# Layer 1's input projection: eight of its fifteen weight blocks by seven half-block products a pair, and its other weights split ahead in layer 0

## The chip, the cores and the metric

One core of a Trainium2 chip runs the whole kernel. The metric is the device time of one execution, in microseconds (us); the figure of a kernel is the median of its runs. The engines are TensorE (PE, matrix products), VectorE (DVE), ScalarE (ACT), GpSimd (POOL) and SyncE (SP). Here SP issues every large transfer, in one queue, and 16 DMA engines carry them out.

## What is computed

The reference is a decoder trunk of two layers over 1024 tokens and 1024 channels, in float32:

```
for l in range(2):
    h = rmsnorm(x, attn_norm[l])
    proj = h @ w_in[l]            # 1824 columns: q, kv and rotary key of a latent attention,
                                  # three parts of a gated convolution, a pooling input,
                                  # q, k, v of a sliding-window attention
    y_a, y_b, y_c, y_d = mla_attention(..), short_gated_conv(..), multiscale_pool(..), swa_sink_attention(..)
    x = x + (concat of the four groups, each rms-normed) @ w_o[l]
    gate, up = split(rmsnorm(x, ffn_norm[l]) @ w_gate_up[l])
    x = x + (silu(gate) * up) @ w_down[l]
return rmsnorm(x, final_norm)
```

## The kernel before

Everything is kept transposed: 128 channels on the partitions, tokens along the row, in two halves of 512 tokens (`HT`), so an activation block is 128 x 512 and there are 8 channel blocks (`NK`). Weights are 128 x 128 tiles.

**Split precision.** TensorE is fed with the type float32r. Each float32 operand is split into a high part (ACT copies and rounds it, L286 or L218) and a low part (DVE subtracts, L287 or L219), and each product is three matmuls, high x high, high x low and low x high, all in `mm3` (L275). So every weight that is used costs one load, one ACT pass and one DVE pass before the matmuls.

**Order of the work, layer by layer.** The mixer stage begins with the input projection: 15 blocks of 128 output columns (q 0-1, k 2, v 3, convolution 4-9, latent q 10-11, latent kv 12, pooling input 13-14) and a small rotary key block. `project` (L460) takes a block's split weights from `weights` (L206), which are loaded one or two blocks ahead through `take` and `ahead` (L249-256), and `proj` (L444) does for each token half 8 x 3 matmuls of 128x512. The evacuation multiplies by the row norm `ratt`, whose rsqrt is known only at the end of the layer before. Between the projections the units of the windowed attention are put (`swa_some`, L666). Then come the latent attention (`keys`, `queries`, `values`, `scores`, `mix_values`), the output projection in parts (`out_some`), and at the end the blocks of `w_o` for the latent group (`wa`, L1318).

**Feed-forward.** Gate and up are already done by Strassen's scheme in Winograd's form: two output blocks, two halves of the channels and two halves of the tokens make a 2 x 2 block product, done with seven half-size products in place of eight. The combinations of activations are made by `combine` (L1132), those of the weights in `GateUp.sums` and `sum4`. A loop at L1523 runs over 22 blocks `f`; each is seven `product` calls of four channel blocks, with DVE and ACT work for the next block woven in. The down projection (loop L1647) is 28 units, seven combinations (`order`, L1423) of four output pairs, each unit 33 matmuls; its weights `dn_raw` are loaded two units ahead, its activations come back from memory (`dn_acts`), and the sums of its weights were made during gate and up by `dn_sums` (L153). At its end `done` (L1612) splits the new `x` into the next layer's `hh`, stores it to `xs`, and adds its squares for the norm.

**Norms.** `SumSq.rnorm` sums squares over the partitions with a matmul by a matrix of ones: in float32 (L345) or, with `parts=True`, split in two float32r matmuls (L340).

**Memory on chip.** Large tiles live in 47 places of 128 x 1024 elements (`Slots`, L56), handed out in program order; a place that is handed out again makes its new writer wait for its last reader.

**What sets the order on each engine.** `arrange` (L1894) is a planner that runs over the program with prices for each instruction and writes out a fixed order for every engine and for SP's queue. The rank of an instruction in the program, moved by the numbers of the table `MOVED` (L2025), is its priority.

Of the kernel before, what the change touches and what calls it, by code (L numbers as in the profile page):

```python
# [55 lines left out]
class Slots:  # L56
# [9 lines left out]

    def pair(self, dt):
# [25 lines left out]
class View:  # L93
# [11 lines left out]

    def ap(self, i):
        assert self.s.dt[i // 2] == self.dt
        return self.s.cur[i // 2][:, i % 2, :]
# [7 lines left out]
def trunk_kernel(ctx: ExitStack, tc: tile.TileContext, ins, out):  # L116
# [26 lines left out]
    nffn = cpool.tile([P, L * NK], F32, name="nffn")  # L143
    act.preload_act_table_set("natural_log_exp_and_others")
# [3 lines left out]
    xr = dpool.tile([NK, P, S], F32, name="xr")  # L148
    ad = [dpool.tile([P, NG * HT], F32, name=f"ad{n}") for n in range(7)]

# [55 lines left out]
    def weights(src, n):  # L206
        if n > 2 * P:
            s = F.pair()
            raw = F.ap2(s)
            sp.dma_start(raw[:, :n], src)  # L210
            hi, lo = (R.ap2(i) for i in ring_next())
            F.free_pair(s)
        else:
            raw = wpool.tile([P, 2 * P], F32, name="vraw", tag="vraw")
            sp.dma_start(raw[:, :n], src)
            hi = wpool.tile([P, 2 * P], F32R, name="vhi", tag="vhi")
            lo = wpool.tile([P, 2 * P], F32R, name="vlo", tag="vlo")
        act.copy(hi[:, :n], raw[:, :n])  # L218
        dve.tensor_tensor(out=lo[:, :n], in0=raw[:, :n], in1=rd(hi[:, :n]), op=ALU.subtract)  # L219
        return hi, lo  # L220

# [17 lines left out]

    def expect_layer(l):  # L240
        for m in ((2, 3, 0) if l else ()) + (4, 5, 6, 1, 13, 14, 10, 11, 12, None, 7, 8, 9):
            if m is None:
                expect(rope_weights, l)
            else:
                expect(weights, ins["w_in"][l, m], 2 * HT)
        for d in range(NK):
            expect(weights, ins["w_o"][l, d, :, 2 * P :], 6 * P)
# [190 lines left out]
    for l in range(L):  # L438
        if l == 0:
            expect_layer(0)  # L440
        sums = dn_sums(l)

# [17 lines left out]
        def project():  # L460
            w = take()
            pp = [proj(w, t) for t in range(2)]
            ahead()
# [29 lines left out]

        if l == 0:
# [12 lines left out]
            for i in range(L):  # L507
                for o, c, n in ((nsink, PC_SINK, 8), (nffn, PC_FFN, NK)):
# [7 lines left out]
        else:  # L516
            wk = take()
            pk = [proj(wk, 0, "s")]
            wv = take()
            pv_ = [proj(wv, 0, "s")]  # L520
            pk.append(proj(wk, 1))
            pv_.append(proj(wv, 1, "s"))
            w = take()
            pq = [proj(w, 0, "s"), proj(w, 1, "t")]
        ahead()
        kk = [[R.pair(), R.pair()] for _ in range(2)]
        for t in range(2):
            f = tmp()
            mul_to(f, pk[t], r_of(t))
            for g, own, oth in ((0, hd, tl), (1, tl, hd)):  # L530
                k1, k2 = R.ap(kk[g][0] + t), R.ap(kk[g][1] + t)
                act.copy(k1[own], f[own])
                act.copy(k1[oth], f[own])
                dve.tensor_tensor(out=k2[own], in0=f[own], in1=rd(k1[own]), op=ALU.subtract)
                dve.tensor_tensor(out=k2[oth], in0=f[own], in1=rd(k1[own]), op=ALU.subtract)
        vs = [[R.half(), R.half()] for _ in range(2)]
        for t in range(2):
            f = tmp()
            mul_to(f, pv_[t], r_of(t))
            p = ps("t")  # L540
            for j in range(4):
                pe.transpose(p[:, j * P : (j + 1) * P], f[:, j * P : (j + 1) * P], ident)
            pv = p.rearrange("p (j g d) -> p j g d", j=4, g=2)
            for g in range(2):
                o = R.ap(vs[g][t]).rearrange("p (j h d) -> p j h d", j=4, h=2)
                act.copy(o[:, :, 0, :], pv[:, :, g, :])
            for g in range(2):
                o = R.ap(vs[g][t]).rearrange("p (j h d) -> p j h d", j=4, h=2)
                dve.tensor_tensor(
                    out=o[:, :, 1, :], in0=pv[:, :, g, :], in1=rd(o[:, :, 0, :]), op=ALU.subtract  # L550
                )

        swa_q(0, pq)
        ytiles("d")
# [126 lines left out]
        def group_scale(g):  # L681

            sg = SumSq(2 * P)
            for t in range(2):
                for c in range(2):
                    sg.add(t, F.ap(y[g][c][t]))
                r = sg.rnorm(t)
# [5 lines left out]
        mixed = {}  # L693

# [10 lines left out]
        def conv(ct):  # L705

            z = F.pair()
            pp = project()
            for t in range(2):
                mul_to(F.ap(z + t), pp[t], r_of(t))  # L710
            yield
            pp = project()
            for t in range(2):
                f = tmp()
                mul_to(f, pp[t], r_of(t))
                mul_to(F.ap(z + t), F.ap(z + t), f)
# [13 lines left out]
            F.free_pair(z)  # L730
            yield
# [8 lines left out]
        for _ in conv(0):  # L740
            swa_some(3)
        swa_q(1, project())


        ytiles("c")
        sw = R.half()
        raw = wpool.tile([P, 2 * P], F32, name="vraw", tag="vraw")
# [1777 lines left out]
```

## Time and profile before

| what | value |
|---|---|
| median of 3 runs | 2054.27 us (2053.95 to 2055.91) |
| the profiled execution | 2055.59 us, of which the span of the trace is 2053.8 us |
| granted TensorE clock | 0.997 of full speed |
| busy: PE, PE's weight loads, DVE, ACT | 2036.9, 1675.5, 1600.7, 981.4 us |
| bytes moved by DMA | 289.74 MB, mean 141 GB/s, 41.8% of the 16 engines' time |
| layer 0's gate and up, down | about 421 to 806 us, 807 to 1016 us of the span |
| layer 1's mixers | about 1016 to 1430 us of the span |

How to read it: an engine's busy time is the part of the span in which at least one of its instructions runs. Matmuls overlap one another, so a single one lasts 389 ns while the next begins long before its end; what one costs is the step from one start to the next. A line number is that of the statement that issues the instruction, and where a helper issues it (L275, L286, L287) the tile names tell the places apart: `u` are the 47 places, `ps_...` are PSUM banks, `in_...` are inputs in memory, and `qd`, `ad`, `xr`, `xs`, `xp` are scratch in memory.

### The profile page before, as it was taken

To read this page: it belongs to the slowest core of one execution; us is meant where nothing else is said; L and a number is where in the kernel's file an instruction comes from. 1 tells how busy PE (TensorE), PEld (TensorE's weight loads), DVE (VectorE), ACT (ScalarE), POOL (GpSimd) and SP (SyncE) were. 2 spreads that over 40 slices of the span, in tenths; PEclk is the share of its full clock that TensorE was granted. 3 is DMA by queue.
4 is the path that set the end of the run, shared out by engine and by line. 5 is a ranking of instruction groups with operands and counts; after the bars stand their busy time and mean duration, and the time that the engine had idled before them with its cause. 6 is when DMAs were issued, how large, how long until landed. Compare 5 with 4: busy or idle time off the path is not lost.

```text
span 2053.8 us, 26024 instructions
## 1 busy us (share of the span) xinstructions
PE 2036.9 (99%) x9418; PEld 1675.5 (82%) x9418; DVE 1600.7 (78%) x2744; ACT 981.4 (48%) x1710; POOL 6.4 (0%) x36
## 2 busy tenths in 40 slices
PE   9999999999999999999999999999999999999998
PEld 7887788888888887888888878887888788888887
DVE  6879988998787877565666898879987778775565
ACT  6447666653333334443543576657333233354342
POOL 0000000000000000000000000000000000000000
PEclk9999999999999999999999999999999999999999
DMA  5020223355445447676411102143564544488462
GB/s 182 24 72 21 74 79 106 123 180 171 164 164 184 164 154 240 225 247 200 156 34 44 47 16 97 55 144 105 176 205 149 174 165 144 161 286 270 149 207 84
DMA packets 149232, 289.74 MB, mean 141 GB/s; under 512 B 12656, under 2 KB 72048, under 8 KB 149104
## 3 DMA queue, kind: packets, MB, share of 16 engines
q1 hardware_dynamic: 149104, 288.08, 41.8%
q8 instruction: 74, 1.21, 0.2%
q14 instruction: 54, 0.44, 0.1%
HBM read 204.67 MB, written 83.36 MB: 140 GB/s over the span
## 4 chain that ended last, share of the span: by engine, by line
PE 94%; DVE 3%; DMA 1%; issue 1%; ACT 0%; SPq 0%; DVEq 0%
PE ps_mm L275 37%; PE ps_s L275 28%; PE ps_t L275 11%; PE ps_pv L275 8%; PE ps_pv L1040 2%; PE ps_t L1028 2%; PE ps_t L345 1%; PE ps_s L975 1%; PE ps_s L977 1%; PE ps_s L976 1%; PE ps_s L567 1%; PE ps_mm L840 1%; PE ps_pv L621 1%; PE ps_t L612 1%; DVE u L287 1%
## 5 line engine op out<-in xcount | busy, mean ns | idle before, releaser
L275 PE MATMUL ps_mm<-u,u 128*128 128x512 f32 (+1 forms) x3376 | 877.0, 389 | 0.0
L275 PEld LDWEIGHTS ps_mm<-u,u 128*128 128x128 f32 x3376 | 617.9, 188 | 129.8 <-issue 6.0
L275 PE MATMUL ps_s<-u,u 128*128 128x512 f32 x2666 | 683.7, 391 | 4.0 <-ACT u L286 1.2
L275 PEld LDWEIGHTS ps_s<-u,u 128*128 128x128 f32 x2666 | 499.4, 188 | 114.5 <-ACT u L286 2.4
L286 ACT CAST u<-u 128x1024 fp32r<-128x1024 f32 (+2 forms) x385 | 335.1, 891 | 456.2 <-DMA u<-ad 86.6
L287 DVE TENSOR_TENSOR u<-u,u 128x1024 fp32r<-128x1024 f32 (+2 forms) x385 | 387.1, 1022 | 154.3 <-ACT u L286 130.4
L275 PE MATMUL ps_t<-u,u 128*128 128x512 f32 (+1 forms) x1122 | 284.2, 378 | 0.5 <-DVE u L1634 0.5
L275 PEld LDWEIGHTS ps_t<-u,u 128*128 128x128 f32 x1122 | 202.2, 188 | 40.2 <-issue 0.7
L275 PE MATMUL ps_pv<-u,u 128*128 128x512 f32 x744 | 204.1, 389 | 0.6 <-ACT u L286 0.6
L275 PEld LDWEIGHTS ps_pv<-u,u 128*128 128x128 f32 x744 | 139.4, 188 | 30.2 <-ACT u L286 1.0
L1386 ACT ACTIVATE tp<-tp 128x512 f32<-128x512 f32 x84 | 52.8, 632 | 92.3 <-DVE tp L357 91.9
L289 ACT ACTIVATE u<-u,par 128x512 fp32r<-128x512 f32 x100 | 70.3, 719 | 39.2 <-DVE u L1177 13.2
L286 ACT CAST u<-ps_t 128x512 fp32r<-128x512 f32 (+3 forms) x128 | 61.0, 501 | 53.0 <-PE ps_t L1028 27.5
L164 DVE TENSOR_TENSOR u<-u 128x256 f32<-128x256 f32 x176 | 73.6, 421 | 15.1 <-DMA u<-in_w_dn 12.6
L287 DVE TENSOR_TENSOR u<-ps_t,u 128x512 fp32r<-128x512 f32 (+3 forms) x128 | 71.4, 576 | 14.7 <-ACT u L286 12.7
L290 DVE SCALAR_TENSOR_TENSOR u<-u,par,u 128x512 fp32r<-128x512 f32 x100 | 73.3, 747 | 6.0 <-ACT u L289 5.8
L321 ACT ACTIVATE tn<-u 128x512 f32<-128x512 f32 (+1 forms) x93 | 52.9, 591 | 35.9 <-DVE u L1634 27.9
L1254 ACT COPY tn<-ps_s 128x512 f32<-128x512 f32 x64 | 37.2, 582 | 66.8 <-PE ps_s L275 59.1
L1387 DVE TENSOR_TENSOR tp<-tp,u 128x512 f32<-128x512 f32 x84 | 57.1, 685 | 10.2 <-ACT tp L1386 9.9
L219 DVE TENSOR_TENSOR u<-u,u 128x1024 fp32r<-128x1024 f32 (+1 forms) x43 | 48.1, 1120 | 18.6 <-PE ps_pv L340 5.8
L218 ACT CAST u<-u 128x1024 fp32r<-128x1024 f32 (+1 forms) x43 | 41.7, 970 | 32.5 <-DMA u<-in_w_in 17.5
L357 DVE TENSOR_TENSOR tp<-tp,u 128x512 f32<-128x512 f32 x84 | 56.9, 684 | 0.3
(191 smaller groups left out, 2006.2 us busy)
## 6 DMA issues: line engine op xcount, KB each, us to landing
u<-in_w_gu SPq DMA_DIRECT2D x88, 512.0 KB, 3.6
ad<-u SPq DMA_DIRECT2D x154, 256.0 KB, 2.2
u<-ad SPq DMA_DIRECT2D x70, 512.0 KB, 4.7
u<-in_w_dn SPq DMA_DIRECT2D x68, 512.0 KB, 3.9
qd<-u SPq DMA_DIRECT2D x44, 512.0 KB, 3.1
u<-qd SPq DMA_DIRECT2D x32, 512.0 KB, 4.8
u<-in_w_in SPq DMA_DIRECT2D x27, 512.0 KB, 3.4
u<-in_xT SPq DMA_DIRECT2D x32, 256.0 KB, 4.5
```

What stands on the lines that cost most here:

```text
L164: dve.tensor_tensor(out=o, in0=o, in1=u, op=ALU.add)
L218: act.copy(hi[:, :n], raw[:, :n])
L219: dve.tensor_tensor(out=lo[:, :n], in0=raw[:, :n], in1=rd(hi[:, :n]), op=ALU.subtract)
L275: pe.matmul(o, w, r, start=start and k == 0 and i == 0, stop=stop and k == n - 1 and i == 2, skip_group_check=again,)
L286: act.copy(hi, f)
L287: dve.tensor_tensor(out=lo, in0=f, in1=rd(hi), op=ALU.subtract)
L289: act.activation(hi, f, AF.Copy, scale=gain)
L290: dve.scalar_tensor_tensor(out=lo, in0=f, scalar=gain, in1=rd(hi), op0=ALU.mult, op1=ALU.subtract)
L321: act.activation(q, f, AF.Square)
L357: dve.tensor_tensor(out=o, in0=a, in1=b, op=ALU.mult)
L1386: last_silu = act.activation(g, g, AF.Silu)
L1387: dve.tensor_tensor(out=g, in0=g, in1=r, op=ALU.mult)
```

## The change

**Four pairs of layer 1's input blocks by seven products.** The blocks 13 and 14, 4 and 5, 7 and 8, 6 and 9 are no longer projected one by one. `paired` does a pair with seven `product` calls of four channel blocks each on `hc`, the combinations of layer 1's input (`combine`, now with the norm of the attention, called by the new `recombine`, which reads `x` back from `xs`). The weights' combinations are made in layer 0's down stage by `prepare_pair`, written to memory, and read back whole and split, three ahead, into three places that are used in turn (`load_unit`, `again`).

**Layer 1's other weights split ahead.** Layer 0's gate and up loop takes `prep()` at three points of each block `f` from 4 to 20: `prepare` loads pieces of layer 1's other seven input blocks, of the rotary block, of `w_o` and of the small weights, splits them and writes both parts to memory. Layer 1 loads the parts (`made_pairs` and others) and does not split them.

**Order of layer 1's mixers.** The seven plain projections come first with all units of the windowed attention between them, then the four pairs, then the latent attention, into which `conv(1)`'s three projections no longer fall.

**Finished groups kept in memory.** The results `d` (windowed attention) and `c` (pooling) are written to `ys` (`spill`) and read back (`fetch`) during the last pair.

**Smaller.** Six norms of layer 1 (groups `d` and `c`, the latent q, two token halves each) use `parts=True`; `combos` reuses two tiles; `MOVED` is new throughout. Layer 0's mixers keep their order.

```diff
+    PLAIN = (2, 3, 0, 1, 12, 10, 11)
+    PAIRS = ((13, 14), (4, 5), (7, 8), (6, 9))
...
+    def prepare(l):
+        def piece(src, n, *outs):
+            s = F.half()
+            raw = F.ap(s)[:, :n]
+            sp.dma_start(raw, src)
+            yield
+            h, lo = R.half(), R.half()
+            split(R.ap(h)[:, :n], R.ap(lo)[:, :n], raw)
+            F.free(s)
+            for i, o in zip((h, lo), outs):
+                sp.dma_start(o, rd(R.ap(i)[:, :n]))
+                R.free(i)
...
+        for m in PLAIN:
+            yield from both(("in", m), ins["w_in"][l, m], 2 * HT, HT)
...
+        for d in range(NK):
+            yield from both(("o", d), ins["w_o"][l, d, :, 2 * P :], 6 * P, 3 * P)
...
+    def prepare_pair(l, m, m2, j, o):
+        s = F.pair()
+        v = F.ap2(s)
+        js = slice(2 * j * P, 2 * (j + 1) * P)
+        sp.dma_start(
+            v[:, :HT].rearrange("p (m n) -> p m n", m=2),
+            ins["w_in"][l, m : m2 + 1 : m2 - m, :, js].rearrange("m p n -> p m n"),
+        )
+        yield
+        a11, a12, a21, a22, q1, q0, s4 = (v[:, k * P : (k + 1) * P] for k in range(7))
+        for w, a, b in ((q1, a21, a22), (q0, a21, a11), (a21, q1, a11), (s4, a12, a21)):
+            dve.tensor_tensor(out=w, in0=a, in1=b, op=ALU.add)
+        h, lo = R.pair(), R.pair()
+        n = 7 * P
+        split(R.ap2(h)[:, :n], R.ap2(lo)[:, :n], v[:, :n])
+        F.free_pair(s)
+        for k, i in enumerate((h, lo)):
+            c = k * HT + j * P
+            sp.dma_start(
+                o[:, :, c : c + P].rearrange("c p n -> p c n"),
+                rd(R.ap2(i)[:, :n]).rearrange("p (c n) -> p c n", c=7),
+            )
+            R.free_pair(i)
...
+        plain_ahead = Ahead(prepare(l + 1) if l + 1 < L else (), 2)
+        pairs_ahead = Ahead(prepare_pairs(l + 1) if l + 1 < L else (), 2)
...
+        def recombine(j, l):
+            v = [[F.half() for _ in range(2)] for _ in range(2)]
+            for n in range(2):
+                for t in range(2):
+                    sp.dma_start(
+                        F.ap(v[n][t]), xs[2 * j + n][:, t * HT : (t + 1) * HT]
+                    )
+            combine(dict(zip((2 * j, 2 * j + 1), v)), hc, j, (0, 1), l, PC_ATTN, natt)
...
+        def load_unit(i=None):
+            if to_load:
+                m, c = to_load.popleft()
+                loaded.append(R.pair() if i is None else R.again(i))
+                sp.dma_start(rd(R.ap2(loaded[-1])), made["pair", m][c])
...
+            def mult(p, b, first=True):
+                i = loaded.popleft()
+                product(p, (R.ap(i), R.ap(i + 1)), hc[b], first, True, not first)
+                R.free_pair(i)
+                load_unit(i)
...
+            g = F.pair()
+            pa, pd = ps("s"), ps("s")
+            mult(pa, B11)
+            act.copy(F.ap(g), pa)
+            mult(pd, B21)
+            out(F.ap(g), pd, 0)
+            mult(pa, N2, False)
+            act.copy(F.ap(g + 1), pa)
+            pc = ps("mm")
+            mult(pc, N1)
+            u = F.pair()
+            act.copy(F.ap(u + 1), pc)
+            mult(pa, T3, False)
+            out(F.ap(u + 1), pa, 1, -1.0)
+            mult(pc, B22, False)
+            out(F.ap(g + 1), pc, 1)
+            mult(pa, T4, False)
+            times_r(F.ap(u), pa, 0, -1.0)
...
+            keys_split(project())
+            values_split(project())
+            swa_q(0, project())
+            ytiles("d")
+            swa_some(3)
...
+            recombine(2, l)
+            rope_keys()
...
+            recombine(3, l)
...
+            for _ in range(3):
+                load_unit()
+            group_scale("d", True)
+            spill("d")
+            wp = made_few(made["pw"], 2 * P)
+            us = paired()
+            pooling(0, us[0], wp)
+            z0, c0 = paired()
...
+            z1, c1 = paired()
...
+            b0, b1 = paired(
...
+            load_few()
+            group_scale("b")
...
+            prep = plain_ahead if f >= 4 and not end else lambda: None
...
         for n, (c, m) in enumerate(units):
-            if n < 5:
-                for _ in range(3):
-                    next(sums, None)
+            pairs_ahead()
...
                 if m == 0:
+                    while pairs_ahead():
+                        pass
                     expect_layer(l + 1)
...
+                if m > 1:
+                    recombine(m - 2, l + 1)
```

`Ahead` with depth 2 starts one job at each call and finishes the one begun two calls earlier.

More of the change, by code (lines that the diff above doesn't have):

```diff
@@ L515, in trunk_kernel @@
                     )
[L516 to L554, printed above, removed]
+            ahead()
+            keys_split(pk)
+            values_split(pv_)
+            swa_q(0, pq)
+            ytiles("d")
         def swa_scores(g, i, p3, nm, rs):
```

602 lines of the change are left out of this document (439 added, 163 removed), and 729 rows, old and new, of the table MOVED.

## The prediction

> **What bounds the kernel now.** I read the page's head first, then its chain, then who waited for whom on TensorE, then the chain in order of time.
>
> ```profile
> span 2053.8 us, 26024 instructions
> PE 2036.9 (99%) x9418; PEld 1675.5 (82%) x9418; DVE 1600.7 (78%) x2744; ACT 981.4 (48%) x1710; POOL 6.4 (0%) x36
> ...
> PE 94%; DVE 3%; DMA 1%; issue 1%; ACT 0%; SPq 0%; DVEq 0%
> ```
> ```profile
> PE ps_s L275 <- ACT u L286: 1.2, 1, 1.2
> PE ps_s L275 <- DVE u L287: 1.2, 1, 1.2
> ...
> PE ps_t L345 <- DVE u L326: 0.2, 1, 0.2
> ```
>
> TensorE is busy for 99% of the span, the chain that ended last runs 94% through it, and all twelve of its waits (the first two and the last are shown) come to some 7.5 us, none above 1.2. Busy time alone would not prove a bound, as overlapping matmuls can hide gaps; the chain's pieces do:
>
> ```profile
> 785.70 5.44 PE ps_t L275 x24
> ...
> 949.30 7.48 PE ps_s L275 x33
> ...
> 1046.77 5.44 PE ps_s L275 x24
> ```
>
> 24 matmuls in 5.44 us and 33 in 7.48 us are 0.2267 us each, in gate and up, in the down stage and in layer 1's projection alike. The two product stages run at this step without gaps. So the time is the number of matmuls, as long as nothing makes TensorE wait; the question of this change is what it saves there and whether its added work brings new waits.
>
> **The change, part by part.**
>
> *Matmuls removed.* A pair of blocks costs 2 blocks x 2 token halves x 8 channel blocks x 3 = 96 matmuls of 128x512. Seven products of 4 channel blocks x 3 are 84. Four pairs save 4 x 12 = 48, at 0.2267 us: **-10.9 us**, all on the path.
>
> The skill would have headroom read otherwise. The Trainium skill, "Perfetto Trace Analysis", section "Identifying the Most-Contended Engine", has TensorE judged by the busy share of its weight loads, which here is 82%; by it there would be slack in TensorE and a saved matmul would be worth less than its step. The even step of 0.2267 us above speaks against it.
>
> *Six norms.* A float32 sum by the matrix of ones goes through in two passes:
>
> ```profile
> 1182.60 0.41 PEld L345 LDWEIGHTS ps_t<-u,ones 128*128 128x128 f32 x2
> 1183.25 0.19 PEld L275 LDWEIGHTS ps_mm<-u,u 128*128 128x128 f32 x1 [0.24 <-issue]
> 1183.68 0.19 PEld L840 LDWEIGHTS ps_mm<-u,u 128*128 128x128 f32 x1 [0.24 <-issue]
> ```
>
> Weight loads otherwise follow at the matmuls' step; behind these passes they come 0.43 us apart, so a norm holds TensorE for 0.86 us. Split in two float32r matmuls it is 0.45. Six times 0.41: **-2.4 us**. The six splits on ACT and DVE are priced below; they lie under projections.
>
> *Weights split ahead, in layer 0's gate and up (blocks f 4 to 20).* `prepare` has 43 jobs: 19 of 512 columns, 16 of 384, 6 of 256, 2 of 128.
>
> ```profile
> core 0: us, PE busy (x) PEld busy (x) DVE busy (x) ACT busy (x) POOL busy (x), PEclk, DMA share, GB/s
> 464.00:787.00 323.00, 323.00 (x1425) 266.85 (x1425) 261.81 (x405) 111.83 (x155) 0.00 (x0) 1.00 0.49 167
> 807.00:942.00 135.00, 134.06 (x591) 110.72 (x591) 78.52 (x94) 55.08 (x67) 0.00 (x0) 1.00 0.68 229
> 942.00:1016.00 74.00, 74.00 (x328) 61.28 (x327) 50.31 (x64) 40.39 (x55) 0.00 (x0) 1.00 0.62 204
> ```
> ```profile
> L287 DVE TENSOR_TENSOR u<-u,u 128x1024 fp32r<-128x1024 f32 x62 | 74.8, 1220 | 21.1 <-ACT u L286 17.3 <-PE ps_pv L275 1.7 <-PE ps_s L275 1.4
> L164 DVE TENSOR_TENSOR u<-u 128x256 f32<-128x256 f32 x88 | 36.7, 420 | 9.2 <-DMA u<-in_w_dn 8.1
> ...
> L287 DVE TENSOR_TENSOR u<-u,u 128x512 fp32r<-128x512 f32 x21 | 14.3, 683 | 1.8 <-ACT u L286 1.8
> ```
> ```profile
> L287 DVE TENSOR_TENSOR u<-u,u 128x384 fp32r<-128x384 f32 x28 | 15.5, 553 | 10.3 <-ACT u L286 10.2
> ```
>
> DVE: 19 x 0.683 + 16 x 0.553 + 6 x 0.420 + 2 x 0.289 (the rows' line carried on to 128) = 25 us. Its 262 of 323 us become 287, 89%. ACT (112 of 323) has room for about as much. Bytes: each job reads its columns once and writes them twice (the rotary job too), 27 MB in all, 84 GB/s more, so the DMA share goes from 0.49 to about 0.74. A block f takes 19 us, its weights are loaded two blocks ahead, and TensorE did not wait once in this window. Cover enough: **0 us**. If DVE's order were bad, each evacuation that comes late would cost TensorE up to its 0.68 us; I keep +2 us for the range.
>
> *Pair weights, in layer 0's down stage.* This is the part that can cost. `prepare_pair` has 16 jobs, each 4 sums of 128 columns and a split of 896 columns: DVE 4 x 0.289 + 1.09 = 2.2 us, 36 us in all. With depth 2 and one call a unit the jobs lie in units 0 to 17, 18 x 7.48 = 135 us, the window 807 to 942 above. There DVE would go from 78.5 to 114 of 135 us, 85%. The DMA is nearer to its limit:
>
> ```profile
> GB/s 355 343 282 344 358 211 399 262 273 58 136 220 300 248 343 308 148 70 138 212 342 408 411 402 266 2 223 162 288 250 310 175 189 138 58 213 1 155 78 68
> DMA packets 12018, 30.87 MB, mean 229 GB/s; under 512 B 1333, under 2 KB 3637, under 8 KB 12009
> ```
> ```profile
> 1248.50:1249.50 1.00, 1.00 (x6) 0.84 (x5) 1.00 (x3) 0.00 (x0) 0.00 (x0) 1.00 0.25 74
> ```
> ```profile
> ACT u L286 <- DMA u<-ad: 31.0, 19, 5.4
> ...
> ACT u L286 <- DMA u<-qd: 13.9, 10, 3.3
> ```
>
> In this window 229 GB/s take a share of 0.68, 337 GB/s for a full share; its 30.87 MB are 92 us of the engines. The jobs' stores go in rows of 512 bytes (128 columns); the nearest row is a microsecond that holds little but a small weight load in rows of 512 bytes, 74 GB/s at 0.25, 296 for a full share. A job reads 0.262 MB (0.78 us at 337) and writes 2 x 0.459 MB (3.10 us at 296): 3.9 us, 62 us for 16. So 154 us of transfer would have to go through 135: 19 us too much if the jobs keep to these units, none if the planner strews them over all 28 (92 + 74 x 0.62 + 62 = 200 of 209 us). The weights are loaded two units, 15 us, ahead, of which a landing takes about 5 (4.8 by a row below); some 10 of the 19 are absorbed. That bounds the stall between 0 and 9 us. What goes late first is ACT's split L286, which already waited 31 us for activations and 14 for sums here, at no cost to TensorE. Each store waits on SP for its split, and behind it in the queue stand the weight and activation loads of the coming units. I take **+3 us**, nearer to the lower end, since the same window already carries landings that come last and TensorE is busy for 134.06 of 135 us.
>
> On the small rows the skill differs: "DMA: Bandwidth & Descriptors", section "Specifications", calls 512 bytes enough for line rate and puts the fabric's ceiling at 435 GB/s. As an estimate from that page the 18.9 MB of the jobs would take 43 us in place of 62, 135 in all, and this term would be 0; slices of the window above do pass 400 GB/s, but the small load ran at 296.
>
> *Two of the four input combinations* (8 DVE operations each, at most 6 us) fall in the last two units, ahead of the new layer's norm; two projections of the first half tokens, 2 x 5.44 us, lie over them: 0.
>
> *Layer 1's mixers.* Gone: about 30 us of DVE splits by the rows above (15 blocks x 1.22, 8 of `w_o` x 0.95, the rest small); come: two combinations, 11 us, evacuations of the pairs and six norm splits, some 15 us. No more than before.
>
> ```profile
> 1052.00:1440.00 388.00, 386.92 (x1873) 313.97 (x1873) 326.23 (x673) 232.83 (x498) 3.08 (x16) 1.00 0.21 69
> ```
>
> A product of a pair lasts 12 x 0.2267 = 2.72 us and reads 512 KB, 193 GB/s, where the DMA share is 0.21 today. Each of three places is filled again only after its product, so a refill has two products, 5.44 us:
>
> ```profile
> u<-qd SPq DMA_DIRECT2D x32, 512.0 KB, 4.8
> u<-in_w_in SPq DMA_DIRECT2D x27, 512.0 KB, 3.4
> ```
>
> Landings of this size take 3.4 us from a quiet stage and 4.8 in a busy one; both fit. Two changes of stage are new: into the pairs (first refills and the combinations for the third product) and into the attention, where three projections, 33 us, no longer cover the first softmax. Nearest rows: the longest waits at such changes, 1.2 us each, so up to +2.4; the 1.1 us that TensorE's 386.92 lacks in this window could also go. I take **+1 us**. Spilled groups and few weights have 76 us of pair products as cover: 0.
>
> Sum on the profiled execution, which took 2055.59 us: -10.9 - 2.4 + 3 + 1 = -9.3, so 2046.3. That execution lies 1.3 us above the median of the runs, 2054.27; for the median, **2045.0**. A change of 0.2%, 4.1 us, is about what a measurement of this kernel can tell from none.
>
> **Rivals.**
>
> - *DMA saturates in the down stage* (ends slower). Place: units 0 to 17; mechanism: 154 us of transfer in 135, SP's fixed order puts stores ahead of the loads. With nothing absorbed, 19 us, and both stage changes at 2.4: 2054.3 - 13.3 + 21.4 = 2062.4. It decides from a stall of about 16 us on. For: the share of 0.68 and ACT's waits. Against: the two-unit lead, and 10 more units with room. Chance 0.09.
> - *The refills come late.* If a landing and its issue take 6.4 us in place of 5.44, about 1 us is lost in every third of 28 products, 9 us: 2054. For: 4.8 in a busy stage. Against: a quiet stage. Chance 0.10.
> - *TensorE is not the bound* (the rule on weight loads): what is saved turns into waiting for DVE, 78% busy; 2054. Against: the even step. Chance 0.03. The rule named above, from "Perfetto Trace Analysis" of the Trainium skill, is this case's only support.
> - *Everything is covered*: -13.3 and no new wait, 2041. For: the planner's order is new and covered all before. Against: full DMA in one stage. Chance 0.11.
>
> The change does what it says: 84 for 96 can be counted in the code.
>
> **How the numbers follow.** The forecast case, 2041.5 to 2050, has 0.67. Faster holds it and full cover, 0.78; same holds late refills and no bound, 0.13; slower the saturated DMA, 0.09. The range goes from 2039.5 (full cover and the 1.1 us) to 2055 (late refills); the saturated case and some edges are left out.
>
> **What would show it.** Right: 48 matmul records fewer, about 9370 (a norm changes two passes for two matmuls); the step still 0.2267; L345 with 12 records fewer; the DMA share in the first 135 us of the down stage at 0.9 or more, with TensorE's new waits there, on L286, near 3 us; pair products in runs of 12 in 2.72 us. Wrong: TensorE waiting more than 10 us in the down stage or at each third pair product, a step above 0.2267 in gate and up, or long gaps ahead of the first pair or the first softmax.

## The result, and the profile after

The changed kernel takes 2070.93 us (2068.83 to 2072.74 in 4 runs) where the kernel before takes 2054.11 beside it (2053.06 to 2055.91 in 4): a ratio of 1.0081, interval 1.0063 to 1.0098. It is slower by 0.8%; the forecast was 2045.0, faster by 0.45%. Its profiled execution took 2070.58 us.

The head of the page and its chain, after:

```profile
span 2068.8 us, 26683 instructions
...
PE 2034.9 (98%) x9370; PEld 1666.7 (81%) x9370; DVE 1646.5 (80%) x2881; ACT 1009.5 (49%) x1773; POOL 6.1 (0%) x36
...
PE 84%; DVE 7%; DMA 6%; issue 1%; ACT 1%; SPq 0%; DVEq 0%; ACTq 0%
```

TensorE has the 48 matmuls fewer (9418 to 9370), yet the span is 15.0 us longer. PE's share of the chain fell from 94 to 84%, and DVE (3 to 7%) and DMA (1 to 6%) came in. Who waited for whom on TensorE, after (engine, tile, line, releaser: us in all, times, longest):

```profile
PE ps_s L448 <- ACT tn L1644: 4.1, 4, 1.8
PE ps_s L448 <- issue: 3.6, 1, 3.6
PE ps_mm L448 <- DVE u L2043: 2.7, 1, 2.7
...
PE ps_s L448 <- DMA u<-pre: 1.1, 1, 1.1
```

Twenty such rows stand where there were twelve, and single waits of up to 3.6 us where none was above 1.2. The table of stretches, after (columns as before):

```profile
464.00:787.00 323.00, 315.88 (x1359) 253.23 (x1358) 266.72 (x431) 125.56 (x189) 0.00 (x0) 0.99 0.74 245
807.00:942.00 135.00, 132.46 (x576) 108.65 (x576) 100.47 (x160) 67.47 (x83) 0.00 (x0) 0.99 1.01 336
1052.00:1440.00 388.00, 382.44 (x1854) 311.63 (x1853) 322.55 (x674) 224.02 (x491) 2.83 (x16) 1.00 0.38 128
```

In the same 323 us of gate and up TensorE begins 1359 matmuls in place of 1425: 66 x 0.2267 = 15 us of work not done there. In the 135 us of the down stage it is 15 matmuls, 3.4 us. The DMA share is 0.74 in the one, as worked out, and 1.01 in the other, above the 0.9 that the prediction asked for.

A finer measure serves for all that follows, the **excess**: for each matmul, the time from its start to the next one's start, less the step of a matmul of its width (0.2267 us for 512 columns; 0.4335 for the two passes of a float32 sum by ones), added up over a stage of the work. It is worked out from all matmul rows of a trace. Stages are cut by work done, as in the kernel before, so they stay comparable when a kernel runs late.

| excess, us | gate and up of layer 0 | down of layer 0 | into layer 1 (1016-1052) | layer 1, 1052-1200 | 1200-1260 | 1260-1440 | rest | sum |
|---|---|---|---|---|---|---|---|---|
| before | 3.0 | 0.1 | 0.0 | 2.1 | 2.1 | 5.0 | 16.6 | 28.9 |
| after | 16.2 | 4.7 | 2.1 | 3.8 | 8.9 | 3.5 | 17.8 | 57.0 |

The sum rose by 28.1; the matmuls and norms that went are worth 13.3; 28.1 - 13.3 = 14.8, the span's 15.0. So the saving is there, and twice as much is lost: 13.2 us in gate and up, 4.6 in the down stage, 6.8 where layer 1 goes from the pairs to the attention, the rest in small places. Some 5 us of the loss are not waits themselves: three times TensorE runs at half its clock for 3.41 us behind a wait (last section). One profile's stage carries some scatter: in the seven profiles whose work in gate and up is the changed kernel's (its own and those of runs 4, 5 and 7 to 10), that excess lies between 14.2 and 19.9. In the down stage the profiles of the changed kernel and of runs 1 to 3 and 7 to 10, with the same work there, lie between 2.5 and 5.2.

What the longest losses in gate and up look like: the chain between 653 and 663 us, after (start, us, what):

```profile
653.27 4.14 DMA pre<-u
...
657.50 1.22 DVE u L460
658.72 0.60 DVE u L1798
659.33 0.34 DVE u L181
659.66 0.60 DVE tp L1789
660.26 1.14 DVE u L460
...
662.83 2.75 DMA pre<-u
```

`pre<-u` is a store of a weight prepared for layer 1. It stands in the chain because DVE's next split (L460) writes into the place that the store still reads. While DVE stands there, the evacuations and sums of the rows below it queue up, and TensorE waits for their banks. The list of what ended DVE's idle time before its splits L460 has the sum, after:

```profile
  ACT u L459: 151.8, 113
  DMA pre<-u: 8.6, 8
```

Eight times a split waited for a store of prepared weights, 8.6 us in all. Waits of this kind are not new, though; the list of the kernel before has one for the stores `ad<-u`:

```profile
  DMA ad<-u: 6.0, 5
```

So the list shows where DVE stood and not what it cost; that takes experiments.

### The profile page after: what moved, and what is told of

Same layout as the page of the kernel before. It is cut to its first block, busy times and chain, and to the rows that moved or that the text cites. A ratio compares the mean times of both kernels' runs of the same rounds, so it can differ in the third digit from the quotient of the medians.

```text
span 2068.8 us, 26683 instructions
## 1 busy us (share of the span) xinstructions
PE 2034.9 (98%) x9370; PEld 1666.7 (81%) x9370; DVE 1646.5 (80%) x2881; ACT 1009.5 (49%) x1773; POOL 6.1 (0%) x36
## 4 chain that ended last, share of the span: by engine, by line
PE 84%; DVE 7%; DMA 6%; issue 1%; ACT 1%; SPq 0%; DVEq 0%; ACTq 0%
PE ps_mm L448 31%; PE ps_s L448 27%; PE ps_t L448 10%; PE ps_pv L448 7%; DVE u L460 2%; PE ps_pv L1465 2%; DMA pre<-u 2%; PE ps_t L1453 1%; DMA u<-in_w_dn 1%; PE ps_s L1400 1%; PE ps_s L1402 1%; PE ps_s L1401 1%; PE ps_t L518 1%; PE ps_s L765 1%; PE ps_mm L1152 1%
## 5 line engine op out<-in xcount | busy, mean ns | idle before, releaser
L448 PE MATMUL ps_mm<-u,u 128*128 128x512 f32 (+1 forms) x3268 | 841.8, 388 | 5.7 <-DVE u L2043 2.7
L448 PE MATMUL ps_s<-u,u 128*128 128x512 f32 x2834 | 725.7, 392 | 11.6 <-ACT tn L1644 4.1
L448 PEld LDWEIGHTS ps_mm<-u,u 128*128 128x128 f32 x3268 | 596.4, 188 | 131.9 <-issue 4.1
L448 PEld LDWEIGHTS ps_s<-u,u 128*128 128x128 f32 x2834 | 530.8, 188 | 132.9 <-ACT tn L1644 7.8
L459 ACT CAST u<-u 128x1024 fp32r<-128x1024 f32 (+4 forms) x453 | 376.3, 853 | 498.7 <-DMA u<-ad 105.9
L460 DVE TENSOR_TENSOR u<-u,u 128x1024 fp32r<-128x1024 f32 (+4 forms) x453 | 435.5, 977 | 162.4 <-ACT u L459 133.2
L448 PE MATMUL ps_t<-u,u 128*128 128x512 f32 (+1 forms) x1094 | 276.8, 380 | 2.6 <-ACT u L459 1.6
L448 PE MATMUL ps_pv<-u,u 128*128 128x512 f32 x744 | 210.1, 390 | 1.0 <-DVE u L460 0.5
L460 DVE TENSOR_TENSOR u<-ps_t,u 128x512 fp32r<-128x512 f32 (+3 forms) x128 | 71.4, 577 | 18.4 <-ACT u L459 17.1
L1465 PE MATMUL ps_pv<-u,u 128*128 128x512 f32 (+2 forms) x184 | 52.4, 360 | 0.0
L1453 PE MATMUL ps_t<-cst,u 128*128 128x128 f32 x288 | 42.9, 275 | 0.1
```

Of the source, the lines that this page charges most:

```text
L448: pe.matmul(o, w, r, start=start and k == 0 and i == 0, stop=stop and k == n - 1 and i == 2, skip_group_check=again,)
L459: act.copy(hi, f)
L460: dve.tensor_tensor(out=lo, in0=f, in1=rd(hi), op=ALU.subtract)
L1453: pe.transpose(p[:, b * P : (b + 1) * P], pr[b][j // 4][:, (j % 4) * P : (j % 4 + 1) * P], ident,)
L1465: pe.matmul(py[:, c0:], v_of(j, h), R.ap(s)[:, c0:], start=j == 0 and n == 0, stop=j == nj - 1 and n == 1,)
```

## The experiments

Two theories stood after this. **Places**: a place stays taken until the stores of the prepared weight have landed, and in-order DVE and ACT stand in front of it. **Traffic or work**: the added transfers (share 0.49 to 0.74, 0.68 to 1.01) or DVE's added splits are themselves too much. A third, **the queue**, belongs beside them: SP takes its transfers in order, so a store whose split is not done holds up the loads behind it. For layer 1, amounts (late transfers, DVE's backlog) stood against the order of the work. All but runs 10, 11 and 12 keep the changed kernel's own order on every engine. The kernel before took between 2053.16 and 2056.05 us beside them.

**1. Gate and up: thin stores.**

```diff
-                sp.dma_start(o, rd(R.ap(i)[:, :n]))
+                sp.dma_start(o[:, :16], rd(R.ap(i)[:, :16]))
```

> The changed kernel with its order on every engine fixed, but the stores of the weights split ahead in gate and up carry 16 columns (all but those of the first block), and layer 1 reads that first block in place of all made weights, so its output is not the reference's. Three theories for the 15 us that layer 0's gate and up lost (1359 matmuls between 464 and 787 us where there were 1425). Places: a place stays taken until its store has landed, and DVE and ACT, in a fixed order, wait for it. Traffic: a DMA share of 0.74 makes every landing late. Work: 25 us more on DVE. Places and traffic expect the stage back: 1410 matmuls or more in that window and 2055 to 2059 us. Work expects no change: 2069 to 2072 us.

2066.25 us, ratio 1.0054 (1.0039 to 1.0069). Excess in gate and up 8.9 us. That is half of the way back: 1397 matmuls in the stretch, not the 1410 that places and traffic expected, and the time is above their 2059.

**2. Gate and up: stores as large, from constants.** The split's places are free as soon as the split is done.

```diff
-                sp.dma_start(o, rd(R.ap(i)[:, :n]))
+                sp.dma_start(o, cst[:, :n])
```

> The changed kernel with its order fixed; the same stores at full size, but out of the table of constants, so no store waits for a split and no place waits for a store (the made weights of layer 1's seven plain blocks, the rotary block, w_o and the small ones are then constants, and the output is not the reference's). Places expects most of the 15 us back: 2055 to 2060 us, 1400 matmuls or more between 464 and 787 us. Traffic and work expect no change: 2069 to 2072 us, 1360 matmuls.

2064.57 us, ratio 1.0043 (1.0028 to 1.0058). Its stretch of gate and up and its row of waits before L460:

```profile
464.00:787.00 323.00, 320.54 (x1397) 259.88 (x1396) 274.33 (x442) 130.49 (x195) 0.00 (x0) 1.00 0.75 249
```
```profile
  DMA pre<-u: 0.6, 1
```

The same traffic (0.75), 38 more matmuls in the stretch than in the changed kernel, an excess of 8.0, and DVE's waits for stores fall from 8.6 to 0.6 us. The thin stores of run 1 did no better than large ones that hold nothing. So the bytes of the stores are not what costs these 8 us.

Such a store holds no place, but neither does it make SP wait for a split. What SP waited for at these stores between 464 and 787 us, in the changed kernel and then in run 1 (run 2 has no such row):

```profile
SPq L327 <- ACT u L459: 35.8, 21, 3.9
SPq L327 <- DVE u L460: 13.4, 22, 1.7
```
```profile
SPq L331 <- ACT u L463: 33.0, 19, 4.7
SPq L331 <- DVE u L464: 12.5, 22, 1.7
```

Run 1 keeps nearly all of this waiting and still gains as much as run 2. So the queue alone is not it either; what both runs have in common is that a place comes back soon after its split. That SP's waits and full-size stores cost something only together is not excluded. The time, 2064.57, lies above the 2060 that places expected, and 5.0 us of excess stay.

**3. The same, with thin splits.**

```diff
-            split(R.ap(h)[:, :n], R.ap(lo)[:, :n], raw)
+            split(R.ap(h)[:, :16], R.ap(lo)[:, :16], raw[:, :16])
```

> As the run before, with stores out of the constants, and the splits ahead on ACT and DVE narrowed to 16 columns (their results are not used). Work expects the gain here and none in the run before: DVE 20 us less busy and 2055 to 2060 us. Places expects what the run before gave, within 2 us. Traffic expects 2069 to 2072 us in both.

2063.74 us, ratio 1.0046 (1.003 to 1.0063). DVE is busy 257.5 us of the 323 in place of 274.3 in run 2, and the excess is 8.2 against 8.0. With the places free, DVE's added work costs nothing that can be seen there; "cover enough" held for it.

**4. Down stage: thin pair stores** (their target is narrowed likewise).

```diff
-                rd(R.ap2(i)[:, :n]).rearrange("p (c n) -> p c n", c=7),
+                rd(R.ap2(i)[:, :16]).rearrange("p (c n) -> p c n", c=1),
```

> The changed kernel with its order fixed; the stores of the pair weights in layer 0's down stage carry one combination of 16 columns, and layer 1 reads the first plain block in place of all made weights, so its output is not the reference's. The prediction's term for saturated DMA there was 3 us, bounds 0 to 9; the trace shows TensorE 576 matmuls in 807 to 942 us where there were 591. If that is the transfers, 2065 to 2068 us, the DMA share of that window back from 1.01 to about 0.75, and the gap of some 4 us near 862 us gone. If the down stage only inherits the lateness of gate and up, no change: 2069 to 2072 us. In neither case does gate and up change.

2067.69 us, ratio 1.0065 (1.0048 to 1.0081). The down stage's excess goes from 4.7 to 0.0 at a DMA share of 0.81. Whether bytes or places did it is left open by this run.

**5. Down stage: pair stores as large, from constants.**

```diff
-                rd(R.ap2(i)[:, :n]).rearrange("p (c n) -> p c n", c=7),
+                cst[:, :n].rearrange("p (c n) -> p c n", c=7),
```

> The changed kernel in its own fixed order; the pairs' stores in layer 0's down stage write constants, as many bytes in the same rows of 512, so that the places of the split weights are free as soon as the split is done; layer 1 reads a made block in place of the pairs' weights, so the output is not the reference's. Thin stores brought the down stage's excess from 4.7 us to 0. If the transfers themselves fill the engines (share 1.01 there), the excess stays at 4 to 5 and the share at 1.0, total 2069 to 2072; if the places held by the stores are the cause, as in gate-and-up, it falls to 1 or less at the same share, total 2065 to 2068.

2069.37 us, ratio 1.0069 (1.0054 to 1.0084), so the total hardly moved; the stage did. Its row:

```profile
807.00:942.00 135.00, 134.74 (x595) 111.11 (x594) 103.78 (x166) 69.40 (x86) 0.00 (x0) 1.00 1.01 342
```

595 matmuls in place of 576, at the same share of 1.01, and an excess of 0.0, outside the 2.5 to 5.2 of the profiles with the pairs' own stores. A DMA system that is full by the profile did not by itself cost TensorE anything. The total shows little of it, above the 2065 to 2068 that places expected, since the next stage, into layer 1, took 4.9 in place of 2.1.

Here, too, two things go at once. Waits between 807 and 942 us: ACT's for a place, then SP's at the pairs' stores, both in the changed kernel, then SP's in run 4:

```profile
ACT u L459 <- DMA pre<-u: 4.3, 1, 4.3
```
```profile
SPq L407 <- ACT u L459: 10.8, 8, 3.5
```
```profile
SPq L407 <- ACT u L459: 10.6, 9, 2.4
```

Run 5 has neither of the first two rows. Run 4 keeps SP's wait and loses nothing, but at a DMA share of 0.81. And the stall itself, in the changed kernel's chain, comes out of a load and not out of a store:

```profile
854.63 8.09 DMA u<-in_w_in
...
863.48 1.70 DVE u L460 x2
...
865.22 4.84 PE ps_t L448 x13
```

The load is one of a pair's raw columns; DVE stands at its sums (L400) until it lands, and TensorE waits for the splits behind them. (TensorE's other wait there, 1.6 us, is for a split on ACT, which itself had stood behind a load `u<-ad`.) In run 5 SP issues this load at 852.68 us. As far as these rows go, held places and the waiting queue made loads late at a full share; that is argued, and which of the two did more is not shown.

**6. All preparation thin**, in gate and up its loads and splits too, in the down stage the pairs' stores.

```diff
-            sp.dma_start(raw, src)
+            sp.dma_start(raw[:, :16], src[:, :16])
```

> The changed kernel in its own fixed order, with all the preparation of layer 1's weights in layer 0 made thin: in gate-and-up the jobs load, split and store 16 columns in place of up to 512 (the first job alone is whole), the pairs' jobs store 16 columns, and layer 1 reads the first made block wherever it read a made one, so its output is not the reference's. Jobs, waits and instructions stay as many, places stay taken as long as the thin transfers need. Until now: storing from a constant brought the excess of TensorE's time over its matmuls' step in gate-and-up from 16.2 to 8.0 us (3.0 before the change), and thin pair stores that of the down stage from 4.7 to 0.0. Theory (the jobs hold their places while loads and stores are under way, loads too): gate-and-up back to about 3, down stage 0, so 2070.9 - 13 - 4.7 = about 2053 to 2056; what then stays against the 2045 forecast is layer 1's mixers and the stage changes, about 10 us. Rival (the rest of gate-and-up comes from the changed order of the stage's own loads and evacuations, or from the waits in the queues, whatever the jobs carry): gate-and-up stays at about 8, 2059 to 2062.

2057.2 us, ratio 1.0022 (1.0012 to 1.0031); gate and up 5.6, down 0.0.

```profile
464.00:787.00 323.00, 321.89 (x1411) 262.70 (x1410) 262.66 (x446) 118.35 (x195) 0.00 (x0) 1.00 0.55 176
```

With the preparation's transfers in gate and up nearly gone, 52 matmuls come back, and the kernel is still slower than the one before by 0.2%: most of what is left lies in layer 1. Neither side's figures came true (about 3 and up to 2056 us; about 8 and 2059 or more). Of the 13.2 us in gate and up some 8 go in run 2, with the stores' hold. The other 5, of which 2.4 go between run 2 and this one, are not explained: steps of 2 to 3 us are no larger than the scatter.

**7. Layer 1: less DVE work.** 44 operations of DVE narrowed; two of them:

```diff
-                dve.tensor_tensor(out=o, in0=p, in1=o, op=ALU.add)
-                times_r(o, o, t, sign)
+                dve.tensor_tensor(out=o[:, :16], in0=p[:, :16], in1=o[:, :16], op=ALU.add)
+                times_r(o[:, :16], o[:, :16], t, sign)
```

> The changed kernel in its own fixed order; in layer 1 alone 44 of DVE's operations (the second and third operation of the pairs' evacuations, the multiplies by the norm's factor, the gate) are narrowed to 16 columns, about 23 us of DVE less between 1052 and 1440 us; the output is not the reference's. Nothing else changes: same instructions, same transfers. Theory (layer 1's stall of 3.6 us at 1240 comes from DVE's backlog, which is busy without a gap from 1204 to 1256): the excess of TensorE's time between 1200 and 1260 falls from 8.9 to about 3, total 2064 to 2066. Rival (late fetches of the kept groups and late refills of the places set it): that excess stays at 8 to 9, total 2069 to 2072.

2069.23 us, ratio 1.0083 (1.0063 to 1.0103). Excess between 1200 and 1260: 7.5 (8.9). The profiles that leave layer 1 as it is (the changed kernel's and those of runs 1 to 6) differ by some 2 us in this stage, so 7.5 is no fall that can be told from none. The backlog as a mere amount is not it.

**8. Layer 1: nothing waits for refills and fetches.**

```diff
-                sp.dma_start(rd(R.ap2(loaded[-1])), made["pair", m][c])
+                sp.dma_start(rd(R.ap2(loaded[-1])[:, :16]), made["pair", m][c][:, :16])
...
-                product(p, (R.ap(i), R.ap(i + 1)), hc[b], first, True, not first)
+                product(p, tuple(R.ap(k) for k in hc[b][0]), hc[b], first, True, not first)
```

> The changed kernel in its own fixed order; in layer 1 the refills of the pairs' weights and the stores and fetches of the kept groups carry 16 columns, the pairs' products take their weights from input combinations that are in memory anyway and the fetched groups are split from constants, so no TensorE, ACT or DVE instruction waits for these transfers; the output is not the reference's. Theory (after the run with less DVE work, which moved the excess of the stage 1200 to 1260 us only from 8.9 to 7.5): late transfers set the stalls at 1226 and 1240 us; the excess of that stage falls to about 4, total 2065 to 2067. Rival (DVE's and ACT's order at the change from pairs to attention, in which two operations on ps_s stand behind others): excess stays at 7 to 9, total 2069 to 2072.

2076.07 us, ratio 1.0098 (1.0083 to 1.0114). Excess between 1200 and 1260: 8.7. The wait of 1.1 us for a refill is gone, but a new one for a split on ACT, ahead of a norm, came up in the stage:

```profile
PE ps_t L513 <- ACT u L459: 2.8, 1, 2.8
```

Without the transfers the loss stays. The total is above the changed kernel's, mostly by stages that this edit does not touch (gate and up 19.5) and by layer 1 before 1200 (7.8 for 3.8); why is not known.

**9. Both together.**

> The run with thin transfers in layer 1's pairs and the one with 44 narrowed DVE operations together; output not the reference's. If the stall at 1240 us is a matter of amount (DVE's work and transfers together), the excess of the stage 1200 to 1260 us falls to the 2.1 of before, total about 2063 to 2065; if it is a matter of the order in which DVE takes the operations, and of TensorE's work that is missing there as cover (the first softmax), it stays at 6 or more, total 2067 to 2070.

2074.13 us, ratio 1.0083 (1.0066 to 1.01); excess 7.8, and the wait of 2.8 us of run 8 is there again. Taken together, the two amounts leave the loss where it was.

**10. Two of DVE's operations earlier.** The order on DVE around 1240 and 2038 us, by line. L1355 is the evacuation of the keys (the expectation calls it the query's), L600 the final scaling.

```diff
+L1355
 L463
 L530
 L463
 L530
-L1355
...
 L600
 L600
+L2043
 L600 (four)
-L2043
```

> The changed kernel, same computation and same order but for two of DVE's operations: at 1243.3 us the evacuation of the query's ps_s bank (L1355) is taken four operations earlier, ahead of the splits of the fetched groups and the sums of squares, and at 2040.4 us the down product's evacuation (L2043) four earlier, behind two of the six final scalings instead of behind all of them. Theory (DVE's order of taking things sets both stalls; the operations moved back have time): the 3.6 us wait at 1240 falls to about 1 and the 2.7 us wait at 2038 to about 0.5, with the half-clock stretches behind them about 5 us in all, 2064 to 2067. Rival (what the moved operation was put behind is itself needed next, the chain of group b's norm and the first scores): the wait at 1240 only moves on, 2 to 3 us from the tail alone, 2067 to 2069.

2070.15 us, ratio 1.0068 (1.0051 to 1.0084). First TensorE's rows at the change of stage in the changed kernel (start, us, engine, line, what, count, idle before and releaser), then the waits of run 10 between 1225 and 1262 us:

```profile
1237.61 2.91 PE L448 MATMUL ps_s<-u,u 128*128 128x512 f32 x12
1244.10 2.87 PE L448 MATMUL ps_s<-u,u 128*128 128x512 f32 x6 [3.58 <-issue]
```
```profile
PE ps_mm L448 <- DVE u L1330: 3.0, 1, 3.0
PE ps_t L518 <- DVE u L499: 1.1, 1, 1.1
PE ps_s L448 <- issue: 1.0, 1, 1.0
PE ps_s L448 <- DMA u<-pre: 0.7, 1, 0.7
```

The wait of 3.6 us shrank to 1.0, and 3.0 and 1.1 came up right behind it, at the next evacuation (L1330) and the next norm (L499): the rival. The excess of the stage is 10.0. At the tail it was the order: the wait of 2.7 us at L2043 fell to 0.5, the excess after 1830 us from 3.4 to 1.2. The total, 2070.15, cannot be told from the changed kernel's 2070.93.

**11. The order planned anew with true prices.** The planner carried every transfer at 400 bytes a ns, and a store's end at its last byte.

```diff
-                wire = max(t + (1000 if v.stores else 1400), wire) + v.size / 400.0
+                wire = max(t + (1000 if v.stores else 1400), wire) + v.wire
-                v.end = wire + 345 if v.stores else wire + 470 + v.size / 1885.0
+                v.end = wire + 345 + v.size / 500.0 if v.stores else wire + 470 + v.size / 1885.0
```

> The changed kernel with nothing changed but the order of its instructions on each engine: its planner prices a transfer by the length of its rows (27 ns for a row of 512 bytes on one of 16 engines, 159 ns for one of 4096, as in the packets of the traces, times 1.15) in place of 400 bytes a ns for all, keeps a place until a store has landed, and new shifts are searched under these prices. In the planner's reckoning the end falls from 2043 us (the old order under the new prices) to 2030; the kernel before stands at 2036.5 there and takes 2054. Theory (the preparation's cost is that of a plan which thought transfers and landings shorter than they are): most of the 13 us of gate-and-up and the 4.7 of the down stage go, total 2046 to 2054. Rival (places, rows and queues cost the same in any order): 2064 to 2071.

2074.35 us, ratio 1.0091 (1.0074 to 1.0108): a miss. Gate and up 12.9, down 4.8, 1200 to 1260 10.0: nothing gained beyond scatter, and layer 0's mixers (12.3 for 7.7) and layer 1's feed-forward (7.6 for 2.7) lost. The reckoning that promised 2030 was wrong by far more than the effect searched for. Nor does a new order heal the change from the pairs to the attention: the planner's own reckoning has gaps of 5.6 us there in the changed kernel's order, and of 5.6 in this one.

**12. The pairs alone.** Layer 1 splits its other weights itself again.

```diff
-        plain_ahead = Ahead(prepare(l + 1) if l + 1 < L else (), 2)
+        plain_ahead = Ahead((), 2)
...
-                expect(made_pairs, made["in", m], 2 * HT)
+                expect(weights, ins["w_in"][l, m], 2 * HT)
```

> The pairs alone: layer 0's gate-and-up prepares nothing, layer 1 loads and splits its other weights itself as before the change; the pairs' weights are still made in the down stage. The computation is the reference's. The order is searched anew under the prices of the re-planned run (2074.35 us), its partner. Theory (the preparation's held places are the cost of gate-and-up): the excess of that stage falls from the partner's 12.9 us to about 3 to 5, while layer 1's mixers gain some 30 us of DVE work and lose 5 to 10 us more at the changes of stage (the planner's own reckoning has gaps of 6 us at 932 and of 12 us between 1210 and 1235); total 2068 to 2078, so no gain either way. Rival (the re-search spoils gate-and-up, whatever is prepared): that stage stays at 10 or more, total above 2080.

2081.82 us, ratio 1.0129 (1.0109 to 1.0148). Gate and up comes down to 6.0 from its partner's 12.9, the way that the theory has it, though not to its 3 to 5. Layer 1 between 1052 and 1440 pays for it, 28.8 for the partner's 16.8, and its feed-forward has 11.1: worse than the 2078 that was the theory's upper end.

## Why the prediction was wrong

**The step that failed** is the term of gate and up, "Cover enough: 0 us", with 2 us kept for the range. It measured 13.2, of which run 2 shows 8 to go with what the stores hold; the rest is open. The prediction asked whether DVE had time (it had: run 3), whether the DMA engines had (they had: 0.74 as worked out, runs 1 and 2) and whether TensorE waited before (it did not). It did not ask how long a job occupies a place. Each job takes half a place for its raw columns and half places for two parts, all from the same 47 that feed the gate-and-up weights, and gives the parts back only when their stores have landed; at such a store SP also waited for the split, some 49 us in this stage. The rows of the landings (last column: median us from issue to landing; the third is of the stores of 512 columns in gate and up, the fourth of the pairs' stores in the down stage), after:

```profile
ad<-u SPq DMA_DIRECT2D x154, 256.0 KB, 3.2
u<-ad SPq DMA_DIRECT2D x70, 512.0 KB, 5.7
...
pre<-u SPq DMA_DIRECT2D x36, 256.0 KB, 3.4
...
pre<-u SPq DMA_DIRECT2D x32, 448.0 KB, 6.3
```

The first two before:

```profile
ad<-u SPq DMA_DIRECT2D x154, 256.0 KB, 2.2
u<-ad SPq DMA_DIRECT2D x70, 512.0 KB, 4.7
```

So not only do the new stores hold places; the old ones hold theirs longer. (In run 2 `ad<-u` still takes 3.1 us, so its longer hold is not in the 8 us that went there.) "A place that is handed out again makes its new writer wait for its last reader" stood in the description of the kernel, and the sum never priced it.

**Matmuls and norms** were right: 48 records fewer, the float32 sums by ones down from 60 records to 48, the step unchanged (the chain of gate and up and of the down stage, after):

```profile
760.85 2.72 PE ps_t L448 x12
...
950.76 19.27 PE ps_s L448 x85
```

19.27 us by 85 is 0.2267 each. The rule of the Trainium skill that the prediction set aside, "Perfetto Trace Analysis", section "Identifying the Most-Contended Engine", would read slack from weight loads that are busy for 81% (it names MFU, the share of the peak rate, beside them); the step did not change, so here it was no slack.

**Pair weights in the down stage**: forecast +3 (0 to 9), measured +4.6. The size was right, the mechanism in part. The prediction had 154 us of transfer in 135 push loads late; the share did reach 1.01 and the stall did come behind a late load, but run 5 keeps that share and loses nothing. So the bytes alone do not do it, and the sum, which counted bytes only, came near by luck; the stores' wait in SP's queue was named and not priced. The Trainium skill, "DMA: Bandwidth & Descriptors", section "Specifications", from which the prediction estimated 0 for the bytes, is borne out in that run in what the bytes cost, but not in the rate that the estimate used: at a share of 1.01 run 5 moved 342 GB/s, well under the page's 435.

**Changes of stage in layer 1**: forecast +1 (up to +2.4), measured +2.1 into the layer and +7.0 from 1052 to 1440, of which 6.8 lie between 1200 and 1260. The place was named (three projections, 33 us, that no longer cover the first softmax), the price was not worked out but taken from single waits of a kernel that still had the cover. Less DVE work, thin transfers, both, two operations earlier and a new order all leave 7.5 to 10 us there, so neither of these amounts sets it alone. Of the 6.8, 1.7 are a stretch at half clock behind the wait of 3.6. What remains is the chain itself, last pair, gates, norm, splits, keys and queries, with little else for TensorE beside it. That is argued from what the runs exclude; moving a projection behind the pairs was not tried.

**The tail**, +2.2 after 1830 us, was in no term. It belongs to the new order and goes with one operation moved (run 10).

**Rivals.** Of the four, only "DMA saturates" ended slower; its stall of 16 to 19 us in the down stage did not come, and the largest loss lay in another stage. Refills hardly came late: TensorE waited for them once, 1.1 us. A rival "places run out" was missing. The lower end of the range, 2039.5, is 0.4 below its own sum (2054.3 - 13.3 - 1.1 = 2039.9), which changes nothing here. None of the versions tried beats the kernel before.

## What to carry to other kernels

Price what a prefetch holds, not only what it moves and computes: place by place, from the load's issue to the landing of the store that reads it, against the places the stage has free. Gate and up had no wait on TensorE and engines to spare, and what the stores held still cost some 8 us there: in-order engines turn one late store into a wait for everything queued behind it. To tell the bytes from what a store holds, store as many bytes from a constant; and as that also frees the queue from waiting for the data, run thin stores of the real data beside it.

## What the runs showed of the hardware that was not expected

After some waits TensorE runs at half its clock, for 3.41 us. TensorE's rows of the changed kernel around a wait of 1.79 us in gate and up:

```profile
748.82 1.07 PE L448 MATMUL ps_mm<-u,u 128*128 128x512 f32 x4
751.68 4.61 PE L448 MATMUL ps_s<-u,u 128*128 128x512 f32 x12 [1.79 <-ACT tn L1644]
```

Twelve matmuls of this width took 2.91 us in the row at 1237.61 above; here they take 4.61, and behind the wait of 3.58 us six take 2.87. The granted clock (the column behind POOL's), ahead of that second wait, behind it, and some microseconds on:

```profile
1238.00:1240.50 2.50, 2.50 (x12) 1.72 (x10) 2.50 (x5) 2.08 (x4) 0.00 (x0) 1.00 0.94 313
...
1245.00:1246.00 1.00, 1.00 (x4) 0.75 (x3) 1.00 (x4) 0.33 (x2) 0.00 (x0) 0.50 0.47 172
...
1247.00:1248.00 1.00, 0.99 (x6) 0.79 (x5) 1.00 (x2) 0.91 (x2) 0.00 (x0) 0.73 0.53 197
```

So a wait can cost 1.7 us more than its own length (4.61 - 2.91, half of 3.41), and the list of waits understates the loss. In the record of the granted clock the changed kernel has three such stretches between its start and its last 10 us, from 752.6, 865.3 and 1244.1 us, each of 3.41 us; the kernel before has one, at 8.7 us. (In runs 1, 11 and 12 one stretch is twice as long.) They are some 5 of the 15 us. The stretch does not follow each wait: behind the 2.74 us at 2038 the clock stayed at 1.00 here and in run 5, while in runs 1 to 4 and 6 to 9 such a stretch begins about where the same wait, 2.73 us there, ends. The Trainium skill, "TensorE: Matmul & The Clock Gate", section "Why this matters for your kernels", asks for no idle gaps above about 3 us; here 1.79 us was enough once, and 2.74 was not always.
